# S5 runs and weight loads begun inside the last pair of column blocks of a streaming encoder layer

## The chip, the cores and the metric

One program on one NeuronCore of a Trainium2 chip. The metric is the device time of one execution in microseconds (us), lower is better. The five engines are named as the profile names them: PE (TensorE, matrix products; PEld is its weight load), DVE (VectorE), ACT (ScalarE), POOL (GpSimd) and SP (SyncE, which here only issues transfers). SP and POOL each issue DMA transfers in the order of their own program; an entry that waits holds up all that stands behind it on that engine.

## What is computed

One layer of a hybrid encoder over 2048 prompt rows and 128 sample rows (8 streams of 16) of width 1024, then a final RMSNorm:

```python
h = rmsnorm(x, ln_g)
u_a, z_a, u_b, z_b, g_a, g_b = split(h @ w_in)      # 512, 512, 1024, 1024, 1024, 1024 columns
y_a = gelu(s5(u_a))                                  # 32 groups of 16 channels, 64 complex states each
y_a = y_a * sigmoid(y_a @ w_glu + b_glu)
p_a = (y_a * silu(z_a)) @ w_pa
y_b = rglru(causal_conv(u_b))                        # gated linear recurrence
p_b = (y_b * silu(z_b)) @ w_pb
out = x + (sigmoid(g_a) * p_a + sigmoid(g_b) * p_b) @ w_out
```

The S5 states, the recurrence states and the last convolution rows are outputs as well.

## The kernel before, in words

Matrix products keep 32-bit accuracy by splitting each operand into a high and a low 16-bit part and adding three products (`passes`, L159 to L163: lines L161, L162 and L163 of the profile are these three). Rows of the input are worked on in five token tiles, `TILES`: four of 512 (n = 0 to 3) and one of 128 (n = 4, the samples).

The program is in four stages that matter here.

1. **The input projection**, in pairs of 128-column blocks (`run_pair`, L1353). A pair is two `quad`s (L828) with the 128 sample columns between them. A quad makes a 2x2 block product with 7 instead of 8 products of 12 matmuls each (`PROD`, L825); its right-hand sides are pages of the input `h` and four formed pages `T1` to `T4`. The quad for tiles 0 and 1 reads the four pages tagged "t0" (`T_1411` to `T_1414`), the quad for tiles 2 and 3 the four tagged "t1". After each of the 15 positions of a pair a hook is called. The last pair (number 15, kind "za") has its own hook, `hook_z` (L1566).
2. **Branch B's recurrence** (`b_work`, L908), on DVE and ACT, beside stage 1. Its results `y` are stored to DRAM (`ybD`) by POOL. Block 7 is the last one.
3. **Projection B**: `Y @ w_pb`, tile by tile, 8 blocks of 24 matmuls of 512 columns for n = 0 to 3 and of 128 columns for n = 4. The weights `wpb` (four pages of 1 MB) go into the "t0" pages; `Y` is `ybD` loaded back (`y_load`, L1556), two loads of 1 MB per tile. Each block is evicted by one DVE instruction that multiplies it with a gate tile `gb` loaded from DRAM. PE takes the blocks from five PSUM banks.
4. **The tail**: GLU (`glu_tile`, products of `yh`), projection A (`pa_tile`, products of `yA`), the output product (`out_tile`, products of `wo` and `M`) and the final norm. `yh` is the S5 result, loaded back from DRAM (`ya` from `yDp`) and split by ACT and DVE (`glu_prep`, L1604).

**Branch A's S5** is 16 tasks `s5_run(q)` (L1408), one for two groups each. A run loads a page `sp` of prepared matrices, `u` and a table; then come 12 matmuls (the front, L1427), a scan on DVE, and for each of the two groups 12 more matmuls (L1472 to L1479), a Gelu on ACT and a store to `yDp` by POOL. The matrices of run q are made earlier by `s5_prep` (L1196), which uses POOL, PE, ACT and DVE and fetches one of its own results back from DRAM (`dd` from `kpD`, on SP). All runs begin only after pair 15. Four can be in flight (`running > 3` makes the fifth wait), one on each "t1" page.

Order is set by hand. Tasks are generators; `pump` (L678) takes steps from them within a budget of estimated DVE time, once per position of a pair (`tick`, or the hook) and twice per block of projection B (`beside`, L1551). Two kinds of background work stop while `busy` (L1128) says so: `NO_SPILL` and `NO_PREP` are ranges of places, and pair 15's position p is place 15 + p. A load that must wait for a page, or for one of the 22 slots tagged "g", waits at its turn on SP's queue. `tail_start` (L1625) loads the four `wo` pages (into "t1") and begins `glu_prep` once every other task is done. Between projection B and the tail stands `while tasks or low or due: beside()`. The GLU weights `wgl` and the first half of `wpa` are loaded into "w" pages in the fourth token tile (`PAGES`, L1643).

There are three "w" pages. Pair 15 uses two of them for its weights; before the change the third is held by `temp` (scratch for the S5 runs, L1584 and `scratch`, L1190) through all of projection B.

Of the kernel before, what the change touches and what calls it, by code (L numbers as in the profile page):

```python
# [8 lines left out]
F32 = mybir.dt.float32  # L9
# [8 lines left out]
P = 128  # L18
# [29 lines left out]
def build(tc, I, O):  # L48
# [3 lines left out]
    def tt(out, a, b, op):  # L52
        V.tensor_tensor(out=out, in0=a, in1=b, op=op)
# [19 lines left out]
    def act(out, a, f, **kw):  # L73
        S.activation(out=out, in_=a, func=f, **kw)  # L74
# [4 lines left out]
    with ExitStack() as es:  # L79
# [5 lines left out]
        def ps(tag, shape=(P, 512)):  # L85
            tag = "a" if tag == "b" else tag
            bufs = {"mm": 5, "a": 3}[tag]
            return psp.tile(list(shape), F32, tag=tag, name="ps_" + tag, bufs=bufs)
# [99 lines left out]
        pga = es.enter_context(tc.tile_pool(name="pga", bufs=1))  # L188

        def page_a(tag, shape, name):  # L190
            return pga.tile([P] + list(shape), F16, tag=tag, name=name, bufs={"h": 6, "w": 3}[tag])
# [5 lines left out]
        hs = pga.tile([P, KB, 2, P], F16, name="hs")  # L197
# [4 lines left out]
        def proj(W, n, tag="mm"):  # L202
            p = ps(tag)[:, :TILES[n][1]]
            gemm(p, W, lambda k: hT(n, k), KB)
            return p
# [9 lines left out]
        with ExitStack() as p1x:  # L215
# [328 lines left out]
            for n in range(4):  # L544
# [8 lines left out]
                for m in range(4):  # L553
                    p = proj(lambda k: wua[m][:, k], n)
# [46 lines left out]
        def page_b(tag, shape, name, dt=F16):  # L601
            return pgb.tile([P] + list(shape), dt, tag=tag, name=name, bufs=4)
# [6 lines left out]
        def gt(shape, dt=F32, name="g"):  # L609
            return gp.tile(list(shape), dt, tag="g", name=name, bufs=slots)  # L610
# [49 lines left out]
        tasks = []  # L660
        low = []
        branch_b = True
        clock = 0
# [460 lines left out]
        prepared = set()  # L1124

        place = 0

        def busy(no):  # L1128

            return branch_b and place in no  # L1130

        NO_SPILL = range(13, 22)
        NO_PREP = range(11, 22)
# [51 lines left out]


        todo = list(range(16))
        temp = None

        def scratch(nm):  # L1190

            if nm == "w":
                return temp[:, 512:1024].rearrange("p (a r c) -> p a r c", a=2, r=2)
            return temp[:, 1024:1280].rearrange("p (r c) -> p r c", r=2)

        def s5_prep(second):  # L1196

            def lags(q, dd):
# [10 lines left out]
            while todo:  # L1209
                while busy(NO_PREP):  # L1210
                    yield Later(1)
# [122 lines left out]
        for n in range(NT):  # L1334
            if n == 1:
                load_states()
            for i in range(2):
                direct(2 + i, n, lambda k: W1[2 * i + k // 4][:, k % 4])
                if n < NT - 1:
                    c = next(wg) if n > 1 else 0  # L1340
# [65 lines left out]
        running = 0  # L1406

        def s5_run(q):  # L1408
            nonlocal running
            while q not in prepared or running > 3:  # L1410
                yield Later(1)
            running += 1
            page = page_b("t1", (2048,), "sp", F32)
            sp, ph = page[:, 0:1536].bitcast(F16).rearrange("p (a x) -> p a x", a=3), page[:, 1536:1792]
            SP.dma_start(out=sp, in_=sD[q])
            u = gt([P, 2, 2, 2, NC], F16, name="u")
# [7 lines left out]
            p = ps("a")[:, 0:272].rearrange("p (g c) -> p g c", g=2)  # L1424
# [8 lines left out]
            n = P  # L1433
            er, ei = (ph[:, o:o + n][:, None, :].to_broadcast([P, 2, n]) for o in (0, P))
            m16_ = m16c[:, q:q + 1].to_broadcast([P, n])
            w, hs_ = scratch("w"), scratch("hs")
            tt(w[:, 0], v[:, :, 0:n], er, MUL)
            tt(w[:, 1], v[:, :, 0:n], ei, MUL)
            tt(hs_[:, 0], w[:, 0, 0], w[:, 1, 1], ADD)
# [28 lines left out]
            for g in range(2):  # L1468
                p = ps("b")[:, 0:272]
                pj = [p[:, 0:NC], p[:, NC:272]]  # L1470
                uf = [u[:, g, b].rearrange("p j c -> p (j c)") for b in range(2)]
                PE.matmul(p, lhsT=dd[:, 0, 2 * g], rhs=uf[0], start=True, stop=False)  # L1472
                PE.matmul(p, lhsT=dd[:, 0, 2 * g], rhs=uf[1], start=False, stop=False)
                for a, b in pas:
                    PE.matmul(pj[1], lhsT=dd[:, 1, 2 * g + a], rhs=u[:, g, b, 0], start=False, stop=False)
                for j in range(2):
                    for a, b in pas:
                        PE.matmul(pj[j], lhsT=wcs[:, a, j, g], rhs=hst[:, g, b], start=False, stop=False)
                PE.matmul(p, lhsT=dd[:, 0, 2 * g + 1], rhs=uf[0], start=False, stop=True)  # L1479
                sc = 1.0 / (VS * WCS)  # L1480
                act(yo[:, g, 0:256].rearrange("p (n j c) -> p j n c", n=4, j=2),
                    p.rearrange("p (j c) -> p j c", j=2)[:, :, 0:P].rearrange("p j (n c) -> p j n c", n=4),
                    AF.Gelu_apprx_tanh, scale=sc)
                act(yo[:, g, 256:272].rearrange("p (j c) -> p j c", j=2),
                    p.rearrange("p (j c) -> p j c", j=2)[:, :, P:NC], AF.Gelu_apprx_tanh, scale=sc)
                r0 = 256 * q + 128 * g
                G.dma_start(out=yDp[:, r0:r0 + P].rearrange("n p x -> p n x"),
                            in_=yo[:, g, 0:256].rearrange("p (n x) -> p n x", n=4))
                G.dma_start(out=yDs[r0:r0 + P], in_=yo[:, g, 256:272])
                running -= g  # L1490
                yield Step(0.6)


# [50 lines left out]
        def page_load(page, src):  # L1544
            SP.dma_start(out=page, in_=src)
            return page

        def wpb_load():
            wpb.append(page_load(page_b("t0", (2, KB, 2, P), "wpb"), wpbD[len(wpb)]))

        def beside():  # L1551
            nonlocal clock
            clock += 1
            pump(2.5)

        def y_load(n):  # L1556
            while (7, n) not in stored:
                beside()
            for h in range(2):
                if n < NT - 1:  # L1560
                    Y[n, h] = page_load(page_a("h", (4, 2, 512), "Y"),
                                        ybD[n, 4 * h:4 * h + 4].rearrange("k p l t -> p k l t"))
                else:
                    Y[n, h] = page_load(hs[:, 4 * h:4 * h + 4], ybS[4 * h:4 * h + 4].rearrange("k p l t -> p k l t"))

        def hook_z(pos, c):  # L1566
            nonlocal clock
            clock += 1
            pump(2.8 - c)
            if pos == 7:  # L1570
                while done["spill"] < 16:
                    clock += 1
                    pump(1e9)
            if 7 < pos < 12:
                wpb_load()
            if pos == 9:
                s5_open()
            if pos == 13:
                y_load(0)

        run_pair(15, hook_z)
        branch_b = False
        temp = pga.tile([P, 2048], F32, tag="w", name="temp", bufs=3)
        s5_init()  # L1584
        def ya_load(m, n):
            if n < NT - 1:
# [45 lines left out]
            for _ in chain(glu_prep(0), glu_prep(1)):  # L1632
                yield Step(1.4)

        for q in range(16):
            tasks.append([clock + 3 * q, s5_run(q)])
        tasks.append([clock, tail_start()])

        def load_w(dst, src):
# [20 lines left out]
        for n in range(NT):  # L1660
            w = TILES[n][1]
            for m in range(8):
# [4 lines left out]
                p = ps("mm")[:, :w]  # L1667
# [5 lines left out]
                g = gbl.pop(0)  # L1673
# [190 lines left out]
```

## Time and profile before

| | us |
|---|---|
| median of 3 runs | 1551.13 (1546.92 to 1555.46) |
| the profiled execution | 1549.53 |
| its span | 1547.7 |
| PE busy | 1446.3 (93% of the span) |
| DVE busy | 1034.2 (67%) |
| ACT busy | 815.5 (53%) |
| POOL busy | 505.3 (33%) |
| mean DMA rate | 144 GB/s |

Times in rows are microseconds from the start of the span. The rows of a timeline give start, duration, engine, line, operation, result and operands, how many instructions were merged, and in brackets how long the engine had been idle before and who ended that. Matmul durations overlap (they are pipelined), so the distance between two starts is what one costs. A PE that runs at the higher of its two clock levels (2.4 GHz) starts a 512-column matmul every 0.22 us.

### The profile page before, as it was taken

Reading aid. Unit: us, or ns where it says so; the run is one execution under the profiler, and the core shown is the slowest. Engines: PE = TensorE matmul, PEld = TensorE weight load, DVE = VectorE, ACT = ScalarE, POOL = GpSimd, SP = SyncE. Lnnn points to the kernel's source line nnn. Section 1 sums busy time; section 2 is a strip of 40 time slices with the busy share of each in tenths; the row PEclk is TensorE's granted clock in tenths of the full one; section 3 lists DMA queues with packets and bytes.
Section 4 is the critical chain, followed back from the end, with each engine's and each line's share of the span. In section 5 each row is a group of like instructions: output and inputs, shape, how many; then the busy total and the mean of one; then the engine's idle time right before and its main releaser. Section 6 shows DMA issues by size and latency. Waiting matters only on the chain.

```text
span 1547.7 us, 22800 instructions
## 1 busy us (share of the span) xinstructions
PE 1446.3 (93%) x8168; PEld 724.0 (47%) x8168; DVE 1034.2 (67%) x1913; ACT 815.5 (53%) x1526; POOL 505.3 (33%) x781
## 2 busy tenths in 40 slices
PE   7999999999899999998898899799999899999998
PEld 4544445444444444444443444355555544454444
DVE  5546768867588686887768777444445696665543
ACT  7642446757577575874856758423222562542322
POOL 0790133444536444274363642223332200000000
PEclk9999999999999999999999999899999899999999
DMA  8325223332423424241333241998766772163521
GB/s 207 106 92 208 89 77 93 102 122 86 140 82 109 130 86 140 76 158 61 104 127 92 87 134 69 324 360 292 251 214 221 265 255 72 70 219 107 177 82 55
DMA packets 168490, 222.21 MB, mean 144 GB/s; under 512 B 39258, under 2 KB 117738, under 8 KB 166328
## 3 DMA queue, kind: packets, MB, share of 16 engines
q1 hardware_dynamic: 144440, 150.96, 30.8%
q0 software_dynamic: 23936, 69.79, 12.0%
q8 instruction: 64, 1.05, 0.3%
q14 instruction: 50, 0.41, 0.1%
HBM read 133.85 MB, written 86.84 MB: 143 GB/s over the span
## 4 chain that ended last, share of the span: by engine, by line
PE 48%; issue 15%; DVE 11%; POOL 10%; ACT 7%; DMA 7%; SPq 2%; POOLq 0%; DVEq 0%; ACTq 0%
PE ps_mm L161 11%; PE ps_mm L163 11%; PE ps_mm L162 11%; PE ps_mm L1773 4%; PE ps_mm L1771 4%; PE ps_mm L1772 4%; DVE xc L65 2%; POOL wt L56 2%; POOL t L56 2%; POOL wc L56 1%; POOL wb L56 1%; DVE wf L65 1%; ACT L74 1%; POOL wraw L56 1%; ACT d L74 1%
## 5 line engine op out<-in xcount | busy, mean ns | idle before, releaser
L161 PE MATMUL ps_mm<-T,wf 128*128 128x512 f16 x512 | 198.8, 388 | 34.8 <-ACT gs L74 23.0
L163 PE MATMUL ps_mm<-T,wf 128*128 128x512 f16 x512 | 198.7, 388 | 1.3 <-DVE wf L65 1.3
L162 PE MATMUL ps_mm<-T,wf 128*128 128x512 f16 x512 | 198.6, 388 | 0.0
L162 PEld LDWEIGHTS <-wf 128*128 128x128 f16 x1232 | 121.7, 99 | 151.3 <-issue 46.2
L161 PEld LDWEIGHTS <-wf 128*128 128x128 f16 x1232 | 121.8, 99 | 121.6 <-issue 12.0
L163 PEld LDWEIGHTS <-wf 128*128 128x128 f16 x1232 | 121.7, 99 | 119.9 <-issue 7.0
L161 PE MATMUL ps_mm<-h,wf 128*128 128x512 f16 x448 | 171.2, 382 | 2.0 <-ACT wf L74 2.0
L163 PE MATMUL ps_mm<-h,wf 128*128 128x512 f16 x448 | 170.8, 381 | 0.7 <-DVE wf L65 0.7
L162 PE MATMUL ps_mm<-h,wf 128*128 128x512 f16 x448 | 170.8, 381 | 0.0
L161 PE MATMUL ps_mm<-Y,wpb 128*128 128x512 f16 x256 | 98.0, 383 | 11.0 <-DMA Y<-ybD 11.0
L65 DVE SCALAR_TENSOR_TENSOR gb<-gb,ps_mm 128x512 f32<-128x512 f32 (+1 forms) x40 | 24.3, 607 | 115.3 <-PE ps_mm L163 115.3
L1773 PE MATMUL ps_mm<-wo,M 128*128 128x512 f16 (+2 forms) x264 | 98.0, 373 | 3.4 <-DVE M L65 3.4
L1771 PE MATMUL ps_mm<-wo,M 128*128 128x512 f16 (+2 forms) x264 | 98.0, 373 | 0.0
L1772 PE MATMUL ps_mm<-wo,M 128*128 128x512 f16 (+2 forms) x264 | 98.0, 373 | 0.0
L162 PE MATMUL ps_mm<-Y,wpb 128*128 128x512 f16 x256 | 98.0, 383 | 0.0
L163 PE MATMUL ps_mm<-Y,wpb 128*128 128x512 f16 x256 | 97.8, 382 | 0.0
L74 ACT ACT_TABLE_LOAD x64 | 82.1, 1283 | 3.7 <-PE ps_mm L163 1.8
L65 DVE SCALAR_TENSOR_TENSOR xc<-ub,PC,xc 128x512 f32<-128x512 f32 x96 | 79.9, 832 | 3.2 <-ACT xc L74 1.0
L65 DVE SCALAR_TENSOR_TENSOR wf<-wraw,wf 128x512 f16<-128x512 f32 (+1 forms) x82 | 64.8, 806 | 6.2 <-ACT wf L74 6.1
L65 DVE SCALAR_TENSOR_TENSOR xo<-ps_mm,xo 128x512 f32<-128x512 f32 (+2 forms) x35 | 23.6, 674 | 65.4 <-PE ps_mm L1773 65.4
L1065 POOL DMA_DIRECT2D gbD<-gs x40 | 21.8, 546 | 134.4 <-ACT gs L74 134.3
L74 ACT ACTIVATE yo<-ps_a 128x256 f32<-128x256 f32 x64 | 14.7, 281 | 86.1 <-PE ps_a L1479 86.0
(323 smaller groups left out, 3529.2 us busy)
## 6 DMA issues: line engine op xcount, KB each, us to landing
wraw<-w_in SPq DMA_DIRECT2D x38, 512.0 KB, 4.4
sp<-sD SPq DMA_DIRECT2D x16, 768.0 KB, 4.9
xt<-x_prompt SPq DMA_DIRECT2D x16, 512.0 KB, 4.2
gbD<-gs POOLq DMA_DIRECT2D x32, 256.0 KB, 2.3
ybD<-y POOLq DMA_DIRECT2D x32, 256.0 KB, 2.8
gaD<-gs POOLq DMA_DIRECT2D x32, 256.0 KB, 2.5
Y<-ybD SPq DMA_DIRECT2D x8, 1024.0 KB, 9.9
gb<-gbD SPq DMA_DIRECT2D x32, 256.0 KB, 6.9
```

The lines of the kernel that those rows point to most:

```text
L56: G.tensor_tensor(out=out, in0=a, in1=b, op=op)
L65: V.scalar_tensor_tensor(out=out, in0=a, scalar=s, in1=b, op0=op0, op1=op1)
L74: S.activation(out=out, in_=a, func=f, **kw)
L161: PE.matmul(p, lhsT=a[:, 0], rhs=b[:, 0], start=first, stop=False, skip_group_check=more)
L162: PE.matmul(p, lhsT=a[:, 0], rhs=b[:, 1], start=False, stop=False, skip_group_check=more)
L163: PE.matmul(p, lhsT=a[:, 1], rhs=b[:, 0], start=False, stop=last, skip_group_check=more)
L1065: G.dma_start(out=dst[m, :, t0:t0 + w], in_=t)
L1771: PE.matmul(p, lhsT=lh[0], rhs=w_[:, 0, c], start=(k == 0), stop=False)
L1772: PE.matmul(p, lhsT=lh[0], rhs=w_[:, 1, c], start=False, stop=False)
L1773: PE.matmul(p, lhsT=lh[1], rhs=w_[:, 0, c], start=False, stop=(k == KB - 1))
```

## The change

- The S5 tasks are put on the list at position 9 of pair 15, to begin 2, 3, 5 and 7 positions later (when the products that read the "t1" pages are through) and then every second position.
- Runs 4, 5 and 6 take "w" pages instead of "t1" pages and do not count in `running`: seven can be in flight.
- `temp` goes; the scratch tiles come from the "g" slots.
- The four `wpb` loads are put at positions 2, 3, 5 and 7 of pair 15 (before: 8 to 11), the first `Y` load at position 8 (before: 13), and the wait for the first 16 spilled weight blocks at position 2 (before: 7).
- From position 7 on, `s5_prep` rests until pair 15 is over.

```diff
@@ -1124,10 +1124,11 @@
         place = 0
+        closing = False
         def busy(no):
-            return branch_b and place in no
+            return branch_b and ((closing and no is NO_PREP) or place in no)
@@ -1185,14 +1186,6 @@
-        temp = None
-        def scratch(nm):
-            if nm == "w":
-                return temp[:, 512:1024].rearrange("p (a r c) -> p a r c", a=2, r=2)
-            return temp[:, 1024:1280].rearrange("p (r c) -> p r c", r=2)
@@ -1407,10 +1400,14 @@
         def s5_run(q):
             nonlocal running
-            while q not in prepared or running > 3:
+            other = 4 <= q < 7
+            while q not in prepared or (running > 3 and not other):
                 yield Later(1)
-            running += 1
-            page = page_b("t1", (2048,), "sp", F32)
+            if other:
+                page = pga.tile([P, 2048], F32, tag="w", name="sp", bufs=3)
+            else:
+                running += 1
+                page = page_b("t1", (2048,), "sp", F32)
@@ -1433,7 +1430,7 @@
-            w, hs_ = scratch("w"), scratch("hs")
+            w, hs_ = gt([P, 2, 2, P], name="hw"), gt([P, 2, P], name="hs")
@@ -1487,7 +1484,7 @@
-                running -= g
+                running -= 0 if other else g
@@ -1564,23 +1561,27 @@
         def hook_z(pos, c):
-            nonlocal clock
+            nonlocal clock, closing
+            closing = 6 < pos
             clock += 1
             pump(2.8 - c)
-            if pos == 7:
+            if pos == 2:
                 while done["spill"] < 16:
                     clock += 1
                     pump(1e9)
-            if 7 < pos < 12:
+            if pos in (2, 3, 5, 7):
                 wpb_load()
             if pos == 9:
                 s5_open()
-            if pos == 13:
+            if pos == 8:
                 y_load(0)
+            if pos == 9:
+                start = [clock + 2, clock + 3, clock + 5, clock + 7]
+                for q in range(16):
+                    tasks.append([start[q] if q < 4 else start[3] + 2 * (q - 3), s5_run(q)])
         run_pair(15, hook_z)
         branch_b = False
-        temp = pga.tile([P, 2048], F32, tag="w", name="temp", bufs=3)
         s5_init()
@@ -1632,8 +1633,6 @@
-        for q in range(16):
-            tasks.append([clock + 3 * q, s5_run(q)])
         tasks.append([clock, tail_start()])
```

What this moves on the engines is shown at three places. Lines of the changed program differ by a few numbers from those before; the names say which instruction is which.

SP's queue inside pair 15 (`wr` is a block of `w_out` to be split, `h0n` the S5 start states, `dd` what `s5_prep` fetches back), before:

```order
L1157 DMA wr<-w_out 128x512 x2
L1545 DMA wpb<-wpbD 128x4096
L1157 DMA wr<-w_out 128x512
L1545 DMA wpb<-wpbD 128x4096
L1397 DMA h0n<-state_s 128x256
L1545 DMA wpb<-wpbD 128x4096 x2
L1157 DMA wr<-w_out 128x512
L1293 DMA dd<-kpD 128x1x256 x4
L1545 DMA Y<-ybD 128x4x1024 x2
L1654 DMA gb<-gbD 128x512 x2
L1415 DMA sp<-sD 128x3072
```

and with the change:

```order
L1158 DMA wr<-w_out 128x512 x2
L1542 DMA wpb<-wpbD 128x4096 x4
L1542 DMA Y<-ybD 128x4x1024 x2
L1158 DMA wr<-w_out 128x512
L1390 DMA h0n<-state_s 128x256
L1412 DMA sp<-sD 128x3072
L1414 DMA u<-uD 128x2x544
L1416 DMA sp<-etD 128x2x128
L1412 DMA sp<-sD 128x3072
L1414 DMA u<-uD 128x2x544
L1416 DMA sp<-etD 128x2x128
L1158 DMA wr<-w_out 128x512
```

The two `Y` loads now stand right behind the four `wpb` loads, ahead of two `wr` loads and of `h0n`; the four `dd` loads that stood ahead of them have gone into projection B; and three S5 runs are loaded ahead of the first `gb`.

SP's queue at the end of projection B, before:

```order
L1545 DMA wt<-wpaD 128x4096
L1654 DMA gb<-gbD 128x512 x4
L1654 DMA gb<-gbD 128x128 x6
L1545 DMA wo<-woD 128x4096
L1654 DMA gb<-gbD 128x128
L1545 DMA wo<-woD 128x4096
L1654 DMA gb<-gbD 128x128
L1545 DMA wo<-woD 128x4096 x2
L1588 DMA ya<-yDp 128x512 x8
```

and with the change:

```order
L1653 DMA gb<-gbD 128x512 x4
L1653 DMA gb<-gbD 128x128
L1542 DMA wo<-woD 128x4096
L1653 DMA gb<-gbD 128x128
L1542 DMA wo<-woD 128x4096
L1653 DMA gb<-gbD 128x128
L1542 DMA wo<-woD 128x4096
L1653 DMA gb<-gbD 128x128
L1542 DMA wo<-woD 128x4096
L1653 DMA gb<-gbD 128x128
L1589 DMA ya<-yDp 128x512 x4
L1653 DMA gb<-gbD 128x128 x3
```

`wo` and `ya` move ahead by five of the eight sample blocks. On PE the last matmul of the last S5 run stood 120 matmuls of 128 columns ahead of the first GLU matmul; now it stands 24 of 512 columns and 192 of 128 columns ahead of it. PE has the same number of instructions in both programs.

DVE at the same place (the eight evictions of the sample blocks, then the low parts `yh` of the GLU input), before:

```order
L65 SCALAR_TENSOR_TENSOR gb<-gb,ps_mm 128x512 x2
L53 TENSOR_TENSOR hh<-hn,hh 128x272
L1460 COPY hst<-hh 64x272 x2
L65 SCALAR_TENSOR_TENSOR gb<-gb,ps_mm 128x128 x8
L53 TENSOR_TENSOR yh<-ya,yh 128x8x32 x16
L69 TENSOR_SCALAR wraw<-wraw 128x1024
```

and with the change:

```order
L1457 COPY hst<-hh 64x272 x2
L65 SCALAR_TENSOR_TENSOR gb<-gb,ps_mm 128x512 x3
L65 SCALAR_TENSOR_TENSOR gb<-gb,ps_mm 128x128 x5
L53 TENSOR_TENSOR yh<-ya,yh 128x8x32 x2
L65 SCALAR_TENSOR_TENSOR gb<-gb,ps_mm 128x128
L53 TENSOR_TENSOR yh<-ya,yh 128x8x32 x2
L65 SCALAR_TENSOR_TENSOR gb<-gb,ps_mm 128x128
L53 TENSOR_TENSOR yh<-ya,yh 128x8x32 x2
L65 SCALAR_TENSOR_TENSOR gb<-gb,ps_mm 128x128
L53 TENSOR_TENSOR yh<-ya,yh 128x8x32 x10
L69 TENSOR_SCALAR wraw<-wraw 128x1024
```

Six of the sixteen `yh` instructions now stand between the last four evictions of projection B, behind the fifth.

## Rows read from the trace of the kernel before

**Rows 1.** PE's waits over the span: total us, times, longest.
```profile
PE ps_mm L161 <- DMA Y<-ybD: 11.0, 2, 9.3
...
PE ps_mm L161 <- ACT yh L74: 4.4, 2, 3.9
```

**Rows 2.** Busy by stretch: PE, PEld, DVE, ACT, POOL, PEclk, DMA share, GB/s.
```profile
960.00:980.00 20.00, 20.00 (x136) 10.65 (x135) 12.95 (x26) 18.07 (x32) 10.08 (x16) 1.00 0.70 255
980.00:1000.00 20.00, 9.00 (x33) 3.66 (x32) 9.30 (x15) 5.04 (x7) 4.50 (x8) 0.74 0.84 297
1000.00:1020.00 20.00, 20.00 (x102) 9.48 (x102) 3.35 (x5) 0.97 (x4) 3.26 (x6) 1.00 1.06 392
...
1220.00:1240.00 20.00, 17.39 (x64) 6.67 (x63) 19.90 (x24) 16.78 (x19) 0.00 (x0) 0.75 0.70 248
```

**Rows 3.** Timeline of PE where pair 15 ends and projection B begins.
```profile
983.59 0.39 PE L172 MATMUL ps_a<-ident,h0n 128*128 128x128 f32 x2
993.31 0.59 PE L161 MATMUL ps_mm<-Y,wpb 128*128 128x512 f16 x1 [9.33 <-DMA Y<-ybD]
...
997.53 0.54 PE L162 MATMUL ps_mm<-Y,wpb 128*128 128x512 f16 x1
...
999.96 0.38 PE L161 MATMUL ps_mm<-Y,wpb 128*128 128x512 f16 x1 [1.67 <-DMA Y<-ybD]
```

**Rows 4.** Timeline of SP's issues in pair 15.
```profile
945.68 0.33 SPq L1545 DMA_DIRECT2D wpb<-wpbD  x1
...
983.86 2.46 SPq L1293 DMA_DIRECT2D dd<-kpD  x4
986.37 1.14 SPq L1545 DMA_DIRECT2D Y<-ybD  x2
```

**Rows 5.** The chain that ended last, around the first Y load.
```profile
987.06 12.86 DMA Y<-ybD
```

**Rows 6.** POOL's store of block 7, tile 0 (timeline).
```profile
961.06 0.54 POOL L980 DMA_DIRECT2D ybD<-y  x1
```

**Rows 7.** DMA issues, 940 to 1214: KB each, median us to landing.
```profile
q1 hardware_dynamic: 25618, 50.43, 54.4%
q0 software_dynamic: 7391, 19.50, 18.7%
...
sp<-sD SPq DMA_DIRECT2D x16, 768.0 KB, 4.9
...
ybD<-y POOLq DMA_DIRECT2D x4, 256.0 KB, 7.0
```

**Rows 8.** Timeline of PE where projection B ends and GLU begins.
```profile
1207.00 0.22 PE L161 MATMUL ps_mm<-hs,wpb 128*128 128x128 f16 x1
...
1213.64 0.22 PE L163 MATMUL ps_mm<-hs,wpb 128*128 128x128 f16 x1
1217.79 0.58 PE L161 MATMUL ps_mm<-yh,wt 128*128 128x512 f16 x1 [3.93 <-ACT yh L74]
...
1229.96 0.38 PE L162 MATMUL ps_mm<-yh,wt 128*128 128x512 f16 x1
...
1283.57 0.39 PE L1773 MATMUL ps_mm<-wo,M 128*128 128x512 f16 x1 [1.92 <-DVE M L65]
```

**Rows 9.** SP's first ya loads, then ACT's and DVE's first yh work (timelines).
```profile
1207.61 10.69 SPq L1588 DMA_DIRECT2D ya<-yDp  x8
...
1215.39 2.34 ACT L74 ACTIVATE yh<-ya 128x256 f16<-128x256 f32 x2 [7.74 <-DMA ya<-yDp]
...
1216.70 2.32 DVE L53 TENSOR_TENSOR yh<-ya,yh 128x256 f16<-128x256 f32 x2 [2.52 <-ACT yh L74]
1219.43 15.46 DVE L53 TENSOR_TENSOR yh<-ya,yh 128x256 f16<-128x256 f32 x14 [0.41 <-ACT yh L74]
```

**Rows 10.** Timeline of PE: one S5 front.
```profile
1018.09 0.87 PE L1427 MATMUL ps_a<-u,sp 128*128 128x136 f16 x12
```

**Rows 11.** Groups on ACT, 1000 to 1214: busy us, mean ns, idle before.
```profile
L74 ACT ACTIVATE v<-ps_a 64x136 f32<-64x136 f32 x64 | 17.8, 278 | 42.8 <-PE ps_a L1427 42.2
```

## The prediction, made before the changed kernel ran

> **What bounds the kernel.** I read PE's waits first. PE is the busiest engine, so a gain has to come out of its idle time or of a time in which another engine sets its pace. Two waits lie where the change works: 11.0 us for the first `Y` of projection B, and 4.4 us for `yh` at the start of GLU [rows 1]. Then the windows. In 1000 to 1020 PE is busy for 20.00 of 20 us at the full clock; in 980 to 1000 for 9.00, at a mean clock of 0.74; in 1220 to 1240 DVE is busy for 19.90 of 20 [rows 2]. So projection B is bound by PE and has no room to give, its entrance is bound by a load, and the start of the tail by DVE. The timelines then say what ends each wait.
>
> *The entrance.* Pair 15's last instruction on PE starts at 983.59 and takes 0.39; the first `Y` product starts at 993.31 and the thirteenth, which needs the second `Y` load, at 999.96. The products up to 997.53 are 0.42 us apart (ten steps in 4.22 us), the lower clock level [rows 3]. `Y` was issued at 986.37, right behind four `dd` loads that began at 983.86 [rows 4], and took 12.86 us to land on the chain that ended last [rows 5]. Its data had been ready long before: POOL issued the store of block 7, tile 0, at 961.06 [rows 6], and in this stretch such a store lands in 7.0 us [rows 7].
>
> *The exit.* The last S5 matmul ends at 1207.00, projection B at 1213.7, and the first GLU product starts at 1217.79 [rows 8]. Between them: `ya` is issued at 1207.61, ACT starts on it at 1215.39, DVE on `yh` at 1216.70, with 16 instructions that end at 1234.9 [rows 9]. At 1283.57 PE still waits for DVE (`M`) [rows 8]; so from 1217 to 1284 DVE's queue, not PE, sets the pace, and the stage ends earlier only if DVE's `yh` work ends earlier.
>
> **The change part by part.** The sum is made on the profiled execution, 1549.53 us; it lies 1.6 us under the median of the three runs, inside their spread, so I give the sum as the time.
>
> *`wpb` and `Y` earlier.* The first `wpb` load goes out at 945.68 in the kernel before too, when the product that reads its page is through [rows 4]. The fourth page is read by the quad's seventh product, five products of 12 matmuls of 0.22 us later: about 959. The first `Y` load stands next on SP's queue and reads older blocks; the second needs the store of block 7, 961.6 + 7.0 = 968.6. From there the landing is bounded by the two loads of before: 6.9 us to the first product's start (986.37 to 993.31) and 13.6 to the thirteenth's [rows 3, 4]. So the second half is there between 975 and 982, the first not later, and PE asks for them at 984.0 and 986.6. The wait goes. Worth: the thirteenth product would start 12 x 0.22 = 2.6 us after 984.0, at 986.6, and not at 999.96: **13.4 us** (9.33 and 1.67 of idle time, the rest half clock). If the load were as late as these bounds allow, nothing of this is lost; if SP were held up in front of it, up to all of it.
>
> *What is late next.* `h0n` and the third `wr` now stand behind `Y`, thus go out near 969; `h0n` is needed at 983.6, and even the slowest landing above (13.6) serves. The first `gb` loads stand behind the third run's page, which frees when the fifth product of the second quad is through, two products or 5.2 us before 983.6; the first eviction needs one 24 matmuls after 984, and PE has five banks, 26 us, before a late eviction stops it.
>
> *S5 begun earlier.* PE's instructions are the same in number, and none of them leaves projection B: the first front moves from 96 matmuls behind B's start to 36. The `s5_prep` work that rests (six small matmuls, five POOL instructions, four `dd` loads) moves from pair 15 into B: nothing, PE is on the path in both places. Cover: every S5 load is issued from 970 on and asked for 36 matmuls (7.8 us) after 984 at the earliest; with 4.9 us to land [rows 7], or with the 13.6 of `Y`, it is there by 984. Without that cover each front would wait as the first `Y` product did.
>
> *Fronts in a row.* With seven runs in flight up to four fronts follow each other on PE, and they share three PSUM banks. A front takes 0.87 us on PE [rows 10], ACT frees its bank with four copies of 0.278 [rows 11]: 2.0 us after its start, when the fourth front would start at about 2.1. Between 0 and, if ACT is late by one run's Gelu work each time, 2 us in all; I take **0.5 us lost**, near the lower end, since the banks just fit.
>
> *S5 finished earlier, GLU.* Call the end of projection B T (1213.7 before). The last S5 matmul ended 6.7 us before T. Now 24 matmuls of 512 columns and 192 of 128 stand behind it: 24 x 0.22 + 192 x 0.056 (119 steps in 6.64 us, [rows 8]) = 5.2 + 10.7 = 15.9 us. `ya` waits for the last `wo` page, freed by that matmul, and follows it by 0.6 us as before: T - 15.3. It landed 7.8 us after its issue (1207.61 to 1215.39) beside the same `wo` loads: T - 7.5, two ACT instructions (2.34) later T - 5.2. DVE's order puts five evictions of B ahead of `yh`; the fifth sample block ends three blocks of 1.34 us before T, so DVE starts at T - 3.7. Sixteen `yh` at 1.10 (15.46 / 14) and three evictions of 0.3 between them: 18.6, until T + 14.9, where it was 1234.9 - 1213.7 = T + 21.2. Shift: **6.3 us**. Everything behind it in DVE's queue up to 1284 follows, and from there on PE is bound by its own work again. Bounds: 0, if `ya` lands as late against T as before; 7, since the fifth eviction holds the start back however early `ya` is. I take 6.3, because `ya` may be 1.5 us later before it costs anything.
>
> *The clock there.* From 1217.79 to 1229.96 PE worked at the lower level: 18 starts in 12.2 us, between short waits for `yh` [rows 8]. I count nothing for it, because DVE sets the pace. The Trainium skill ("TensorE: Matmul & The Clock Gate", Part 1: The HAM clock gate) says that half rate is the default and that activity releases it; by that page PE would still be at the lower level while it is fed in pieces, and the sum stays as it is unless that lasts (rival C).
>
> **Sum:** 1549.5 - 13.4 - 6.3 + 0.5 = **1530.3**, so 1530.
>
> **The rivals.**
>
> A. *GLU starts no earlier against T.* For it: `ya` stands right behind four `wo` loads of 1 MB on SP's queue and took 7.8 us to land [rows 9]; six `yh` now stand ahead of three evictions. Against: 9 us more lead. Then 1549.5 - 13.4 + 0.5 = 1536.6.
>
> B. *The change does not bring `Y` forward*: some wait stands in front of it on SP's queue (a "g" slot of one of the two `wr` loads ahead of the four `wpb`). Against: the first `wpb`, behind those same `wr`, went out at 945.68 [rows 4]. Then 1549.5 - 6.3 + 0.5 = 1543.7.
>
> C. *PE becomes the bound at the start of the tail.* At half clock throughout, the 96 GLU products of the first two tiles end 96 x 0.42 = 40 us after T; before, they ended at 1229.96 + 77 x 0.22 = 1246.9, 33 after T. Then the 6.3 is gone and up to 7 more: 1537 to 1544, and I take 1537. Against: before, full clock was back after 12.2 us, with longer waits than are now expected [rows 8].
>
> D. *Slower: the transfers become the bound where B starts.* SP's queue up to the second tile's `Y` holds four `wpb`, four `Y` loads of 1 MB, 0.5 MB of sample `Y`, five S5 runs of 1.2 MB (768 KB [rows 7], and 272 and 128 by their shapes), and 2.4 MB of small loads: 17.4 MB from 946 until that `Y` is asked for at 1025, 220 GB/s; POOL's queue (q0) moved 19.50 of 69.9 MB [rows 7], which makes it 305 GB/s in all. In 1000 to 1020 the engines moved 392 [rows 2], so a fifth is spare. If the rate granted fell under 305, fronts and the second `Y` would wait on PE, in order, and each wait like the one removed costs 13.4: two of them make 1530.3 + 26.8 = 1557; the point of change is a loss of 19 us. The Trainium skill ("DMA: Bandwidth & Descriptors", Bandwidth) puts the limit of one core's HBM traffic at about 358 GB/s; by that page only a seventh would be spare and this rival would deserve more, but the 392 of this trace speak against such a limit here.
>
> **How the numbers follow.** The forecast 0.73, A 0.11, C 0.06, B 0.05, D 0.05. A measurement of this kernel can tell about 0.5% (7.8 us) from no change, so "faster" means under 1543.4 and "slower" over 1558.9. The forecast, A and C are faster (0.90); B lies on the border, and I put half of it and some of D on "same": faster 0.92, same 0.05, slower 0.03. The range reaches down to 1523 (7 instead of 6.3, no loss in the fronts, and the spread of the runs, 5 us, against me) and up to 1541 (A and C with the 2 us of the fronts and the same spread in part); it leaves out B and D.
>
> **What would show it.** In the changed kernel's profile: `Y` issued on SP before 970 and no wait `Y<-ybD` on PE over 1 us; PE at 1.00 clock through B's first 20 us; the first front about 8 us behind B's first product, without idle time; at B's end the first `yh` of DVE before the last `gb` evictions, and the 16th about 15 us after B's last product; PE's wait for `yh` under 2 us in the first place. The prediction is wrong if PE waits for `sp` or `u` at a front, if DVE stands idle in front of the first `yh` while evictions queue behind it, or if PE's later waits for `M` grow by what the entrance gave.

## The result, and the profile after

| | before | after |
|---|---|---|
| median of the runs | 1551.02 us (1546.92 to 1555.46, 4 runs) | 1532.24 us (1531.49 to 1532.98, 4 runs) |
| ratio, 95% interval | | 0.9878 (0.9851 to 0.9906) |
| profiled execution | 1549.53 us | 1532.98 us |

The change makes the kernel 1.2% faster; the time lies 2 us over the forecast and inside its range. PE's waits in the changed kernel, over the whole span (total, times, longest):

```profile
PE ps_mm L161 <- ACT gs L74: 23.2, 11, 5.8
...
PE ps_a L1267 <- POOL wc L56: 4.5, 4, 2.0
PE ps_mm L1772 <- DVE M L65: 3.4, 2, 1.9
PE ps_mm L162 <- DVE yh L53: 3.3, 3, 1.5
```

The wait of 11.0 us for `Y` [rows 1] is not among them, nor is any for `sp`, `u` or another load in projection B. Its entrance on SP's queue, then on PE:

```profile
949.27 13.79 SPq L1542 DMA_DIRECT2D wpb<-wpbD  x4
963.11 10.55 SPq L1542 DMA_DIRECT2D Y<-ybD  x2
973.76 0.50 SPq L1158 DMA_DIRECT2D wr<-w_out  x1
974.36 0.39 SPq L1390 DMA_DIRECT2D h0n<-state_s  x1
```

```profile
986.01 0.39 PE L172 MATMUL ps_a<-ident,h0n 128*128 128x128 f32 x2
986.23 0.38 PE L161 MATMUL ps_mm<-Y,wpb 128*128 128x512 f16 x1
986.45 0.38 PE L162 MATMUL ps_mm<-Y,wpb 128*128 128x512 f16 x1
```

The first half of `Y` is issued 23 us ahead of its first product; before, it was issued 2.8 us behind the start of pair 15's last work [rows 3, 4]. The second half waits on SP's queue for the store of block 7, as the prediction had it, goes out at 973.29 and has 15.5 us until the thirteenth product asks for it at 988.82 (the queue's waits, 940 to 1000):

```profile
SPq L1542 <- DMA ybD<-y: 9.7, 1, 9.7
```

PE goes from `h0n` to the first product without a gap, at steps of 0.22 us. The windows (columns as in rows 2: length, PE, PEld, DVE, ACT, POOL busy, PE's granted clock, DMA share, GB/s) against the same stretches of before [rows 2]:

```profile
980.00:1000.00 20.00, 20.00 (x105) 9.63 (x103) 15.07 (x24) 9.29 (x16) 9.20 (x14) 1.00 1.04 376
1000.00:1020.00 20.00, 20.00 (x143) 11.25 (x141) 13.56 (x50) 10.38 (x28) 4.85 (x9) 1.00 1.06 391
1220.00:1240.00 20.00, 18.27 (x87) 8.34 (x85) 19.62 (x39) 9.15 (x16) 0.00 (x0) 1.00 0.68 220
```

The exit, on SP, ACT, DVE and PE; the last sample product ends at 1203.96, which is T from here on (1213.86 before, from its last product of 0.22 us at 1213.64 [rows 8]):

```profile
1188.98 6.80 SPq L1589 DMA_DIRECT2D ya<-yDp  x4
...
1195.79 2.40 ACT L74 ACTIVATE yh<-ya 128x256 f16<-128x256 f32 x2 [7.24 <-DMA ya<-yDp]
...
1200.19 2.46 DVE L53 TENSOR_TENSOR yh<-ya,yh 128x256 f16<-128x256 f32 x2
...
1207.37 11.04 DVE L53 TENSOR_TENSOR yh<-ya,yh 128x256 f16<-128x256 f32 x10
```

```profile
1203.80 0.38 PE L161 MATMUL ps_mm<-yh,wt 128*128 128x512 f16 x1
...
1205.08 0.38 PE L162 MATMUL ps_mm<-yh,wt 128*128 128x512 f16 x1 [0.26 <-DVE yh L53]
...
1207.42 0.38 PE L162 MATMUL ps_mm<-yh,wt 128*128 128x512 f16 x1 [1.52 <-DVE yh L53]
...
1209.76 0.38 PE L162 MATMUL ps_mm<-yh,wt 128*128 128x512 f16 x1 [1.53 <-DVE yh L53]
```

GLU now starts on PE at once, and DVE is through with its sixteen `yh` at 1218.41, T + 14.5, where it was T + 21.0 [rows 9].

**Stage by stage.** Three cuts divide each profiled execution: a product of pair 15 that waits 0.36 us for `gs`, the eviction of an earlier product by ACT (946.00 before, 949.59 after); the transposes of `h0n` behind pair 15; T.

| stage, us | before | after | difference |
|---|---|---|---|
| to the cut in pair 15 (the work up to there is the same) | 946.00 | 949.59 | +3.59 |
| from there to the transposes | 37.59 | 36.42 | -1.17 |
| transposes to T (B) | 230.27 | 217.95 | -12.32 |
| T to the end of the run | 335.67 | 329.02 | -6.65 |
| sum | 1549.53 | 1532.98 | -16.55 |

The stages that the change touches give 20.1 us; this profile hides 3.6 of them, because the profiled run came late to pair 15 (a second profile of the same kernel, after_again below, has this cut at 946.82). The medians differ by 18.8.

### The profile page after: what moved, and what is told of

Read it like the earlier page. It is cut to its first block, busy times and chain, and to the rows that moved or that the text cites. A ratio compares the mean times of both kernels' runs of the same rounds, so it can differ in the third digit from the quotient of the medians.

```text
span 1531.2 us, 22814 instructions
## 1 busy us (share of the span) xinstructions
PE 1445.1 (94%) x8168; PEld 725.6 (47%) x8168; DVE 1033.3 (67%) x1913; ACT 816.0 (53%) x1526; POOL 504.8 (33%) x781
## 4 chain that ended last, share of the span: by engine, by line
PE 48%; issue 16%; DVE 11%; POOL 10%; ACT 8%; DMA 5%; SPq 2%; POOLq 0%; DVEq 0%; ACTq 0%
PE ps_mm L161 11%; PE ps_mm L163 11%; PE ps_mm L162 11%; PE ps_mm L1772 4%; PE ps_mm L1770 4%; PE ps_mm L1771 4%; POOL t L56 2%; POOL wt L56 2%; DVE xc L65 2%; POOL wc L56 1%; DVE yh L53 1%; POOL wb L56 1%; ACT d L74 1%; DVE wf L65 1%; ACT L74 1%
```

## The experiments

The question after the result: which of the three edits (loads of `wpb` and `Y` early; the preparation of S5 rests from position 7; S5 early with seven runs in flight) brings which part. The table holds all kernels; its stages are cut as above, in each kernel's profiled execution (times in us); medians and ratios are against the kernel before on the same chip (its medians there: 1551.02 beside the first result, 1551.58 for loads_early to four_in_flight, 1555.73 for y_before_dd to yh_in_b, 1552.62 for the last three).

| kernel | median | ratio, 95% interval | wait for Y | B | T to end | 16th yh |
|---|---|---|---|---|---|---|
| before | 1551.02 | | 11.0 | 230.27 | 335.67 | T + 21.0 |
| after (the changed kernel) | 1532.24 | 0.9878 (0.9851 to 0.9906) | 0 | 217.95 | 329.02 | T + 14.5 |
| loads_early | 1542.00 | 0.9929 (0.9906 to 0.9952) | 0 | 216.82 | 336.95 | T + 20.7 |
| s5_early | 1544.24 | 0.9944 (0.9923 to 0.9965) | 10.9 | 231.22 | 329.10 | T + 14.6 |
| prep_rests | 1539.89 | 0.9917 (0.9892 to 0.9941) | 0.9 | 219.22 | 336.53 | T + 20.6 |
| four_in_flight | 1538.01 | 0.9905 (0.9881 to 0.9929) | 0 | 217.96 | 334.68 | T + 20.0 |
| y_before_dd | 1542.02 | 0.9914 (0.9892 to 0.9935) | 2.3 | 219.32 | 336.37 | T + 20.4 |
| no_rest | 1543.98 | 0.9938 (0.9917 to 0.9960) | 0 | 222.10 | 337.38 | T + 20.1 |
| yh_at_once | 1531.83 | 0.9850 (0.9827 to 0.9872) | 0 | 217.96 | 327.17 | T + 12.3 |
| yh_in_b | 1528.70 | 0.9841 (0.9817 to 0.9864) | 0 | 220.91 | 323.78 | T + 5.8 |
| after_again | 1530.83 | 0.9864 (0.9845 to 0.9884) | 0 | 217.96 | 329.15 | T + 14.6 |
| yh_in_b_wo_early | 1522.90 | 0.9810 (0.9794 to 0.9827) | 0 | 217.96 | 319.26 | T - 0.1 |
| s5_late_seven | 1547.63 | 0.9963 (0.9946 to 0.9979) | 0 | 219.87 | 342.16 | T + 25.8 |

### The loads alone: loads_early

To the kernel before, in `hook_z`:

```diff
-            if pos == 7:
+            if pos == 2:
                 while done["spill"] < 16:
...
-            if 7 < pos < 12:
+            if pos in (2, 3, 5, 7):
                 wpb_load()
...
-            if pos == 13:
+            if pos == 8:
                 y_load(0)
```

Expected: 

> The kernel before with the loads of wpb and Y alone brought forward; S5 and its preparation stay where they were. Two gains that add (my theory): the entrance gain needs only Y's place on SP's queue, so all of the 13.4 us comes and nothing of the exit's 6.6: about 13.4 us under the kernel before, no wait of PE for Y, the last S5 matmul still 6.7 us before the end of projection B and the 16th yh of DVE still about 21 us after it. Rival, S5 is what helps (its runs ahead of the block keep PE or the queues in order): under 5 us, with a wait for Y, or one for sp or dd in its place.

B is 13.45 us shorter, the exit as before, as my theory had it. The whole gave 9.6 and not 13.4: pair 15 is 1.2 longer (a new wait of 1.08 for `gs`) and the time behind T is 1.3 more (its clock; see no_rest).

### S5 alone: s5_early

To the changed kernel, the three lines above the other way round. Expected: 

> The changed kernel with the loads of wpb and Y put back to their old places in pair 15; S5 early, seven in flight, preparation resting. My theory: the exit's 6.6 us stay (16th yh about 15 us after the end of projection B). Y stands behind the second wr, which went out at 976.6 in the kernel before, and without dd in front it goes out near 978; by the two landings of before (6.9 and 13.6 us) its second half is 4 to 5 us late: a wait of that length, with some half clock. So 13 to 16 us under the kernel before, 4 to 7 over the changed one. Rival, only an earlier issue of Y takes the entrance wait away: 6.6 us under the kernel before and the wait of 11 us whole. Rival, the S5 loads ahead of Y on SP's queue wait for their pages and hold Y longer than dd did: slower than the kernel before.

The exit's gain is whole (329.10), and the entrance's is gone to the last microsecond: the wait stayed whole, as the first rival had it, and not at 4 to 5 us. SP's queue and PE:

```profile
979.34 0.33 SPq L1158 DMA_DIRECT2D wr<-w_out  x1
981.23 3.77 SPq L1542 DMA_DIRECT2D Y<-ybD  x2
```

```profile
994.74 0.58 PE L161 MATMUL ps_mm<-Y,wpb 128*128 128x512 f16 x1 [10.94 <-DMA Y<-ybD]
```

With two S5 runs' loads in front of it, `Y` went out at 981.2, and already its first half took 13.5 us. I had given that half 6.9, its price beside fewer loads. So the early S5 needs the early loads: taken alone, it puts its own transfers where `dd` stood.

### The rest of the preparation alone: prep_rests

To the kernel before:

```diff
+        closing = False
...
-            return branch_b and place in no
+            return branch_b and ((closing and no is NO_PREP) or place in no)
...
+            closing = 6 < pos
```

Expected: 

> The kernel before with one thing changed: the preparation of S5 rests from position 7 of pair 15, so that no dd load stands ahead of Y. The dd loads waited 6.8 us for the store of kpD with Y behind them. If that is the cause of the late Y (my theory for the larger part of the wait): Y is issued near 977 and not at 986.4, its second half is 4 us late, and 6 to 9 us of the 13.4 come. Rival, Y's own place (position 13) is what is late: under 3 us. Exit as before, 16th yh about 21 us after the end of projection B.

More came than expected: `Y` was issued at 968.1, PE waited 0.9 us for it, and B is 11.05 us shorter although it now holds the preparation's small matmuls. In the kernel before, three long waits of SP's queue stood ahead of `Y` (the queue's waits, 960 to 990). The first held the queue until 967.32, in front of three of the `wpb` loads; the other two stood between the last `wpb` and `Y`:

```profile
SPq L1157 <- DVE y L53: 21.2, 1, 21.2
SPq L1293 <- DMA kpD<-kf: 6.8, 1, 6.8
SPq L1157 <- DMA woD<-wq: 6.7, 1, 6.7
```

Of the two behind `wpb` I had taken only one away, that of `dd`. In this kernel the `wr` load did not wait for the store of `wq` either and stood on the queue right before `Y`:

```profile
967.72 0.33 SPq L1158 DMA_DIRECT2D wr<-w_out  x1
968.11 1.67 SPq L1546 DMA_DIRECT2D Y<-ybD  x2
```

### Y one position earlier: y_before_dd

To the kernel before: `if pos == 12:` instead of 13 for `y_load(0)`. Expected: 

> The kernel before with one call moved: the load of Y at position 12 of pair 15 instead of 13, so that it stands behind the fourth wpb and ahead of the second wr and of the four dd loads. Nothing else moves: S5's preparation still runs in pair 15. Theory 1 (what is late is the dd loads' wait for kpD and the wr's wait for woD, with Y behind them on SP's queue): Y is issued near 970, PE's wait for Y is under 1 us, about 13 us less than the kernel before up to the end of projection B, exit as before (16th yh about 21 us behind it). Rival (what counts is the work of the preparation on POOL, which delays the stores): Y still lands after 984 and more than half of the wait stays.

`Y` went out at 972.7, ahead of `wr` and `dd`, which then waited 4.8 and 7.9 us without harm. PE waited 2.3 us for it, not under 1: the first product came 15.9 us after the issue. SP, then PE:

```profile
972.69 1.82 SPq L1545 DMA_DIRECT2D Y<-ybD  x2
```

```profile
988.56 0.38 PE L161 MATMUL ps_mm<-Y,wpb 128*128 128x512 f16 x1 [1.69 <-DMA Y<-ybD]
```

B is 10.95 us shorter. So the cause of the late `Y` is shown from three sides: whatever frees it from the two waits between `wpb` and itself (its load put five positions earlier, or one, or the preparation resting) takes 9 to 11 of the 11 us away. The wait of 21.2 us further ahead is still there in this kernel.

### The change without the rest: no_rest

`closing` taken out of `busy` in the changed kernel. Expected: 

> The changed kernel without the rest of S5's preparation (the flag closing never acts). Y stands ahead of dd by its own early place, so theory 1 says: no wait for Y, entrance as in the changed kernel. The order of the program shows 144 products of 128 columns behind the last S5 matmul instead of 192 and 24 of 512, as with four in flight: by the exit's theory the 16th yh ends 20 us behind projection B and not 14.5, so 5 to 6 us over the changed kernel. Rival, the rest is needed at the entrance (dd stands ahead of the third run's sp and holds it, and fronts wait): a wait for sp or u on PE, 8 us over or more.

The exit is lost as expected. But B is 4.1 us longer too: the first S5 run's second part waits on PE.

```profile
1016.33 0.52 PE L1475 MATMUL ps_a<-hst,sp 128*128 128x136 f16 x6 [3.14 <-DVE hw L53]
```

My theory had no such wait, and the rival had the place but not the way. The four `dd` loads, which no longer stand ahead of `Y`, now stand ahead of the third run's `sp` and of the first gate tiles `gb`, and wait 6.0 us for the store of `kpD` with these behind them. So the first eviction of B is late, and DVE, idle for 9.1 us, comes to the first S5 run's scan (`hw`) only behind it. SP, then DVE:

```profile
992.70 2.72 SPq L1286 DMA_DIRECT2D dd<-kpD  x4
...
997.27 2.55 SPq L1653 DMA_DIRECT2D gb<-gbD  x2
```

```profile
1006.55 0.69 DVE L65 SCALAR_TENSOR_TENSOR gb<-gb,ps_mm 128x512 f32<-128x512 f32 x1 [9.11 <-DMA gb<-gbD]
```

The scan's first instruction starts 10.1 us after the run's front (1008.36 and 998.24); in the changed kernel it is 4.1 (998.11 and 994.00). Then 2.1 us of the preparation's copies on ACT stand ahead of the run's own, whose first ends at 1016.3, where PE's wait ends (the view puts the wait down to DVE's `hw`; these times speak for ACT's `hst`):

```profile
1013.70 2.13 ACT L74 ACTIVATE d<-dd 128x512 f16<-128x512 f16 x2
1015.85 0.88 ACT L74 ACTIVATE hst<-hh 64x272 f16<-64x272 f16 x2
```

Most of the rest of the 4.1 us is the clock behind that wait: 0.61 was granted in 1016 to 1020. How much of the wait is `gb`'s and how much ACT's was not tried apart.

Pair 15 is 2.3 longer (the wait of 1.00 for `gs` again, and the small matmuls). The time behind T is 2.7 more than with four in flight, at the same T + 20, and that is the clock too: in both kernels PE waits 1.5 and 1.9 us for `M`, 66 to 69 us behind T, but here it then falls to the lower level and takes 0.43 us for each of 13 products, 2.7 us more than at the higher one. The windows with the second of these waits, here and with four in flight:

```profile
1280.00:1284.00 4.00, 2.85 (x7) 1.04 (x8) 3.93 (x7) 0.86 (x2) 0.00 (x0) 0.50 0.36 93
```

```profile
1268.00:1272.00 4.00, 2.67 (x13) 1.26 (x14) 3.93 (x7) 0.69 (x2) 0.00 (x0) 1.00 0.31 82
```

### Fewer in flight, or later: four_in_flight, s5_late_seven

To the changed kernel: `other = False`, and for the second the sixteen `tasks.append` behind `run_pair(15, hook_z)` instead of at position 9. Expected: 

> The changed kernel with four S5 runs in flight, none on the pages of the pairs' weights; S5 still begins inside pair 15. In its order 144 products of 128 columns (8.0 us) stand behind the last S5 matmul, where the changed kernel has 192 of 128 and 24 of 512 (15.9 us). My theory, the exit follows the last S5 matmul: ya lands 7.5 us later against the end of projection B, yh starts about 5 us later, the 16th ends about 19.6 us after the end of projection B: 4 to 5 us over the changed kernel, 15 under the kernel before. Rival, an early start is enough and the number in flight is not: within 1.5 us of the changed kernel.

> The changed kernel with its S5 runs, seven in flight, begun only behind pair 15. Its order puts the last S5 matmul right ahead of the first product of GLU, with none of projection B's behind it (the kernel before: 120 of 128 columns). Theory: entrance as in the changed kernel (no wait for Y, 218 us from pair 15's end to the end of B); the exit follows the last S5 matmul: ya issued at the end of B and landed 8 us later, two ACT instructions, 17.6 us for 16 yh: 16th yh about 28 us after the end of B, 7 us later than in the kernel before, so 13 to 14 us over the changed kernel. Rival, seven in flight gives the exit's gain without the early start: within 2 us of the changed kernel.

With four in flight the exit is 5.7 us later, the entrance untouched. SP, then DVE:

```profile
1193.03 10.19 SPq L1589 DMA_DIRECT2D ya<-yDp  x8
```

```profile
1203.00 17.64 DVE L53 TENSOR_TENSOR yh<-ya,yh 128x256 f16<-128x256 f32 x16 [2.07 <-ACT yh L74]
```

`ya` is issued at T - 7.6 and DVE stands idle until ACT has made the first high parts, behind all of B's evictions. Begun late with seven in flight, S5 ends where B ends, and PE waits for the whole chain behind it:

```profile
1213.27 0.58 PE L161 MATMUL ps_mm<-yh,wt 128*128 128x512 f16 x1 [8.36 <-ACT yh L74]
```

The time behind T is 342.16, 13.1 over the changed kernel's. B is 1.9 longer than the 218 expected, with a wait of 2.2 us for `wc` of the preparation on PE. So the exit needs all three parts, the early start, seven in flight and the rest: without any one of them the 16th `yh` is back at T + 20 or later.

That the 16th `yh` sets the time behind T can be read off the table. Take the 335.67 us of the kernel before, subtract by how much the 16th `yh` came earlier, and add what the lower clock behind the waits for `M` cost (2.7 us in no_rest, 1.7 in loads_early, 1.4 to 1.5 in prep_rests, y_before_dd and s5_late_seven, nothing in the others): for all kernels but yh_in_b and yh_in_b_wo_early this gives the time behind T to 0.3 us. Those two are 1.7 and 4.7 us longer than that, so there the 16th `yh` no longer sets it; in the last, PE has 1.3 us of waits left behind T.

### DVE's yh, and a faster kernel

Two runs ask whether those 16 `yh` bound the tail. The first writes each low part at once (`low()` for `defer(1, low)` in `glu_prep`). Expected: 

> The changed kernel with the low part of each yh written right behind its high part instead of a beat later, which puts two evictions less ahead of DVE's first yh. Theory: in the changed kernel the place in DVE's order holds the start (DVE idle 1 us between evictions from T - 9, T the end of projection B, while ya has landed at T - 8.0 and ACT is through with the first pair at T - 5.6); DVE starts near T - 5.6, ACT's 16 (1.1 each) then set the pace, the 16th yh ends near T + 11 instead of T + 14.5, and PE's waits for yh (3.3 us) shrink to about 1: 2 to 4 us less. Rival, ya sets the start: no change.

The 16th ends 2.1 us earlier and the time behind T is 1.9 us less, at the edge of the 2 to 4 expected. PE's waits for `yh`, `yA` and `M`, all DVE's, are 5.6 us together (1.0, 3.7, 0.9), where they were 8.4 and 8.5 in the two profiles of the changed kernel: part of what `yh` gave went into the wait for `yA`, since DVE has the same work to do. The medians alone could not show so little. The second makes `yh` inside B:

```diff
+        def glu_early(ns):
+            while not opened:
+                yield Later(1)
+            for n in ns:
+                yh[n] = page_a("h", (4, 2, TILES[n][1]), "yh")
+            for m in range(4):
+                while not finished.issuperset(range(4 * m, 4 * m + 4)):
+                    yield Later(1)
+                for n in ns:
+                    ya[m, n] = ya_load(m, n)
+                yield Later(3)
...
-            for _ in chain(glu_prep(0), glu_prep(1)):
-                yield Step(1.4)
```

(`finished` holds the S5 runs that are through; `opened` is set in the third token tile, when two pages are free; the lines left out are the copies and subtractions of `glu_prep`.) Expected: 

> The changed kernel with ya and yh of the first two token tiles made in projection B: the four channel groups each as soon as the four S5 runs that write it are through, instead of all eight groups behind the last run. If DVE's 16 yh behind the end of B are what bounds the start of the tail, they go from there (12 of 16 stand ahead of the last sample products in DVE's order): PE has no wait for yh (3.3 us), does not fall to the lower clock there (some 1.7 us), and the waits for yA and M (5.1 us) shrink too: 5 to 10 us less than the changed kernel. Rival, the tail is bound by PE alone, or by DVE's later work: under 2 us. Rival, the eight ya pages held early slow the last S5 runs: slower.

The tail gave 5.2 us and B took 3.0 back, so that 2.3 of the expected 5 to 10 were left. DVE, in its last evictions, and PE behind it:

```profile
1202.46 0.29 DVE L65 SCALAR_TENSOR_TENSOR gb<-gb,ps_mm 128x128 f32<-128x128 f32 x1 [5.82 <-DMA gb<-gbD]
```

```profile
1206.33 0.22 PE L161 MATMUL ps_mm<-hs,wpb 128*128 128x128 f16 x1 [1.98 <-DVE gb L65]
```

The last `ya` loads waited 23.1 us on SP's queue for the last S5 run, with the four `wo` loads and the last `gb` loads behind them in turn (the queue's waits, 1165 to 1210):

```profile
SPq L1591 <- DMA yDp<-yo: 23.1, 1, 23.1
```

So the next run issues each `wo` load as soon as its page is free:

```diff
-            while len(finished) < 16 or done["spill"] < 44:
-                yield Later(1)
             for i in range(4):
+                while len(finished) < 13 + i or done["spill"] < 32 + 4 * i:
+                    yield Later(1)
```

(and the last `ya` loads stand behind the fourth). Expected: 

> The changed kernel with ya and yh made in projection B as in the run before, and each wo load on SP's queue as soon as the S5 run whose page it takes is through, ahead of the last ya loads. In the run before the last ya loads waited on SP's queue for the last S5 run with all four wo loads (4 MB) behind them, gb loads landed late behind those, and PE waited 2.4 us for the evictions of gb. Theory: those 2.4 us go, the tail stays at 324 us behind the end of B (5 under the changed kernel): 5 to 6 us less than the changed kernel, 2 to 3 less than the run before. Rival, the late gb are due to the other traffic there: no better than the run before.

Both came: B is back at 217.96, and the time behind T is 9.9 us less than the changed kernel's, where 5 had been expected; the 16th `yh` ends at T - 0.1 and not at T + 5.8. `ya` now waits 2.6 us on the queue and not 23.1, so whether it was this wait or the `wo` loads' traffic that made `gb` late is not told apart. PE works through 1200 to 1220, where it stood 3.3 us in the changed kernel, and of the waits from there to 1400 one is left:

```profile
1200.00:1220.00 20.00, 20.00 (x180) 12.58 (x178) 14.95 (x30) 7.42 (x11) 3.23 (x6) 1.00 0.81 282
```

```profile
PE ps_mm L1797 <- DVE M L65: 1.3, 1, 1.3
```

It takes 1522.90 us beside 1530.83 of the changed kernel on the same chip (ratios to the kernel before 0.9810 and 0.9864, intervals apart), and so beats both kernels. The changed kernel was run again for that: 

> The changed kernel itself, beside the next two on the same chip. Ratio to the kernel before as at first, 0.985 to 0.991; from the end of projection B to the end 329 us, the 16th yh 14.5 us after the end of B.

 It gave 0.9864, 329.15 us behind T and the 16th `yh` at T + 14.6.

## Why the prediction was right, point by point

- **wpb and Y earlier, 13.4.** From the transposes of `h0n` to the thirteenth product 16.37 us before [rows 3], 2.81 now: 13.6. Shown by loads_early alone. The mechanism holds, but I named only one of the two waits between `wpb` and `Y`: that of `dd`; the `wr` in front of it had lost as much (6.7 beside 6.8 us). Block 7's store held the second half as foreseen: it went out at 973.29, which is 969.7 without the 3.59 us by which this profile is late; I had 968.6.
- **The rest of the preparation, "nothing".** As a cost that was right: pair 15 became 1.17 us shorter, and B holds about as much more. As a part of the change it was the step I read least well. Alone it is worth the entrance (prep_rests), and in the change both ends hang on it (no_rest): the entrance because `dd` then holds `gb`, the exit because S5's order ends later without it.
- **What is late next.** Nothing was: PE has no wait for a load in B. The landing of `sp` rose from 4.9 [rows 7] to a median of 9.5 us and had cover enough. The first front starts at 994.00, 7.8 us after the first product, as counted.
- **Fronts in a row, 0.5 lost.** Not seen. B's 12.32 is 13.6 less about 1.2 for the small matmuls, which leaves 0.0; the lower bound was right.
- **S5 finished earlier, 6.3.** 6.65 measured. Last S5 matmul T - 16.2 (foreseen T - 15.9), `ya` issued T - 15.0 (T - 15.3), ACT at T - 8.2 (T - 7.5), DVE's first `yh` T - 3.8 (T - 3.7), the 16th T + 14.5 (T + 14.9). That the place in DVE's order and not `ya` holds the start is borne out by yh_at_once.
- **The clock.** PE's step was the lower level's only from 1210.40 to 1213.80, behind the waits of 1.52 and 1.53 us, not for 12 us as before [rows 8]. In those 3.4 us eight products took 0.43 us each instead of 0.22: 1.7 us, for which I had counted nothing (and 19 products start in the 12.2 us of before, not 18). It cost nothing, as DVE set the pace there: the time behind T fell by 6.65 us where the 16th `yh` came 6.5 earlier. What I had not seen is that the clock can fall again behind the waits for `M`, where it does cost (no_rest).
- **The rivals.** A (GLU no earlier) is what four_in_flight and no_rest do: it comes if S5's last matmul has 8.0 us of products behind it and not 15.9 (three blocks fewer, one of 512 columns and two of 128), and I gave it 0.11. B did not come; `Y` began to go out at 963.1. C fell with the short stretch at the lower clock. D did not come: 376 and 391 GB/s at the entrance without a wait. The Trainium skill ("HBM Reference", Specifications) says that a core that streams alone goes well above the share of 358 GB/s that it has beside its neighbour, up to about 425. These windows of a kernel on one core agree: both lie over 358. The limit that I weighed in rival D is the one for two cores.
- **The sum.** -19.2 foreseen, -20.1 in the stages concerned, -18.8 between the medians.

Two statements of "what would show it" failed in their wording. "`Y` issued before 970" holds for its first half alone. The other is PE's wait for `yh` under 2 us in the first place. The first wait is 0.26, but three make 3.3 us; DVE still bound that stretch, which is where the faster kernel found its gain.

## What to carry to other kernels

When a load is late, read what stands in front of it on the queue that issues it, every wait of it, and not only the transfer: here any one of three edits freed it, so their gains do not add, and only undoing them one by one showed which the others need. A wait that stays on the queue falls on the next load behind it: in no_rest `dd` held `gb` in place of `Y`. A producer that ends earlier pays through the engine that takes over its result; when that engine has 18 us of such work in one piece, making it in portions as each part of the input is complete gains more than shifting it. Compare runs by stage: the cut times here agree to 0.1 us where totals of one kernel spread by 5 or more.

## What the runs showed that I had not expected

- In these profiles the spread arises ahead of the change: the two profiles of the changed kernel differ by 2.7 us in all and by 2.8 at the cut in pair 15. The product that begins the first stage cut starts between 944.06 (prep_rests) and 953.07 us (yh_at_once), with the same work of PE ahead of it, while B took 217.95 or 217.96 us in five profiled executions (after, its second run, four_in_flight, yh_at_once, yh_in_b_wo_early).
- The first half of `Y` took 13.5 us (s5_early) and 15.9 us (y_before_dd) from its issue to its first product, twice the 6.9 of the kernel before [rows 3, 4]: with all loads on one queue, a landing time of one order was no price for another.
- Bringing the `wpb` and `Y` loads forward without the rest costs pair 15 a new wait of 1.0 us for `gs` (loads_early and no_rest); in the kernels where the preparation rests it is not there.
